# A hybrid pooling and attention layer: which scores share the PSUM banks of the row maxima

## The chip, the cores and the metric

The kernel runs on one core of one Trainium2 chip. The metric is device microseconds of one launch, taken as the median of several runs; times of one kernel agree within about 0.3%. Beside the timed runs there is one profiled execution, whose trace is read below. Times in it count from the start of its span.

## The reference, cut to what matters

One encoder layer over 1024 tokens of width 1024, in 32-bit floats. A normalised and modulated input is projected once; half of the columns go through a multi-scale mean pooling, the other half through latent attention with 8 heads, and both are joined by an output projection and added to the input. The part that the change touches is the attention of one head:

```python
def attend(qblk):
    s = jnp.einsum('bqhd,bkhd->bhqk', qblk, k, preferred_element_type=jnp.float32) * scale
    p = jax.nn.softmax(s, axis=-1)
    return jnp.einsum('bhqk,bkhd->bqhd', p.astype(v.dtype), v)
```

Queries and keys have 96 elements per head (64 without and 32 with rotary position), values 64. All 1024 positions attend to all 1024.

## The kernel before, in words

**Stages.** Until about 225 us the kernel makes the modulation, the latent projections, the pooling and the gates. From 225 to 409 us it runs the attention, in one loop over 64 jobs written out in the order in which each engine is to work (nothing is reordered by a scheduler here). From 409 us to the end it makes the rest of the output projection.

**Jobs.** A head has eight jobs, called slots here: job i belongs to head i // 8 and slot i % 8. Slots 0 to 3 (hf = 1, j = 0 to 3) each take 128 queries of the second half against all 1024 keys. Slots 4 to 7 (hf = 0, j = 0 to 3) each take 256 keys against the 512 queries of the first half, already turned round. A tile name carries the head, hf and j: `st210` is the score tile of head 2, slot 0; `st200` that of head 2, slot 4.

**One job.** Its scores are six matmuls into one PSUM tile of two banks: `scores(i, 0)` and `scores(i, 1)`, lines 800 and 804. In slots 0 to 3 DVE then takes the row maximum (lines 808 and 809). In the next turn of the loop ACT computes the exponential (line 819). For most jobs this goes to SBUF, and the PSUM tile is free when it is done. For slots 1 and 7 the exponential is written back into the PSUM tile, ACT makes its 16-bit high part (line 824) and DVE the low part (line 831), both from PSUM; only then is the tile free, about two turns after its scores. In the other slots POOL makes the low part. Six turns after the scores PE multiplies by the values (`attend`, lines 849 and 850); after slots 3 and 7 of a head ACT copies the sums out (`out_copy`, line 868) in slots 1 and 5.

**Row maxima.** Slots 4 to 7 have keys on the partitions, so their row maxima are needed ahead, for 512 queries of the next head. `prep_max` does this four times per head: two matmuls into a tile `rs` (line 730), and one DVE reduction (line 733). For heads 1, 2, 3, 5 and 7 the four stand at the ends of slots 4 to 7 of the head before; for heads 4 and 6 at the ends of slots 5, 6 and 7 of the head before and of slot 0 of the head itself. At slot 4 of heads 3, 5 and 7 an output transpose `yt` (line 887) takes the same banks first.

**PSUM.** The eight banks are shared by three pools: `stp`, two score tiles (four banks); `avp`, one tile of sums (two banks); `rsp`, one tile (two banks) for the row maxima, the transposes and, by line 793, one score tile per head. A tile that is put where another lay waits until the last reader of that one is done. `rsp` has one place, so there the tile before is always the one that is waited for. In `stp` the one of the two places that is taken is fixed when the program is built.

**Waits stand in line.** PE executes its matmuls in the order of the program. A matmul that waits for its PSUM banks holds everything behind it, other heads' sums and row maxima included.

Of the kernel before, what the change touches and what calls it, by code (L numbers as in the profile page):

```python
# [29 lines left out]
TWO_PI_PARTS = (6.28125, 0.001934051513671875, 1.255422830581665e-06, 2.430839973754928e-10)  # L30
INV_2PI = 0.15915494309189535
INP = (1, 7)
XH = 6
XS = (4, 5)
XS2 = (2, 2)
# [23 lines left out]
def body(ctx, tc, small, cond, xT, ada_sc, ada_sh, ada_gt, w_lat, w_fm, pool_w, w_uq, w_ukv, gains, pos, w_out, out):  # L59
# [148 lines left out]
    with ExitStack() as pa:  # L208
# [29 lines left out]
        for k in range(NK):  # L238
            pool, tag = (wp, "raw") if k in (0, 1, 6, 7) else (mp, wu_tags[k - 2])
# [508 lines left out]
    stp = ctx.enter_context(tc.tile_pool(name="psS", bufs=2, space=PSUM, reuse_waits="tile"))  # L748
    avp = ctx.enter_context(tc.tile_pool(name="psV", bufs=1, space=PSUM, reuse_waits="tile"))
    rsp = ctx.enter_context(tc.tile_pool(name="psR", bufs=1, space=PSUM, reuse_waits="tile"))  # L750
# [39 lines left out]
    def scores(i, n):  # L790
        h, hf, j = jobs[i]
        if n == 0:
            pool, tag = (rsp, "r") if h and hf and j == 1 else (stp, "st")
            stt[i] = pool.tile([P, 2, 512], F32, tag=tag, name=f"st{h}{hf}{j}")
        qh_, ql_ = qs[h]
        kh_, kl_ = ks[h]
        if hf == 0:
            kt = j * 2 + n
            for a, (l, r) in enumerate(((kh_, qh_), (kh_, ql_), (kl_, qh_))):
                T.matmul(stt[i][:, n], l[:HW, kt * P:(kt + 1) * P], r[:HW, 0:512], start=(a == 0), stop=(a == 2))  # L800
            return
        qt = 4 + j
        for a, (l, r) in enumerate(((qh_, kh_), (qh_, kl_), (ql_, kh_))):
            T.matmul(stt[i][:, n], l[:HW, qt * P:(qt + 1) * P], r[:HW, n * 512:(n + 1) * 512],  # L804
                     start=(a == 0), stop=(a == 2))
        if n:
            bps[i] = ep.tile([P, 1], F32, tag="bp", name=f"bp{h}{j}")
            V.tensor_reduce(bps[i], stt[i], AX.XY, ALU.max)  # L808
            V.tensor_scalar(bps[i], bps[i], nesc, 6.0 * LN2, ALU.mult, ALU.add)  # L809
# [16 lines left out]
    def in_psum(i):  # L826

        return i % 8 in INP and (i > 7 or i == 7)

# [118 lines left out]
    def at(h, step, f, *a):  # L948
        extra.setdefault((h, step), []).append((f, a))
# [3 lines left out]
    for n in range(2):  # L953
        for part in range(2):
            for d in range(2):
                at(XH + d, XS[part] + XS2[d] * n, out_split, d, (n,), (part,), G)

# [47 lines left out]
    for i in range(len(jobs) + LAG + 1):  # L1005
        live = i < len(jobs)
        h, step = i // 8, i % 8
# [14 lines left out]
        if live:  # L1022
            scores(i, 0)
# [27 lines left out]
        if live:  # L1051
            scores(i, 1)
# [141 lines left out]
```

## Time and profile before

| | |
|---|---|
| median of 3 runs | 501.46 us (501.36 to 502.86) |
| the profiled execution | 500.05 us, its span 498.3 us |
| PE, DVE, ACT, POOL busy over the span | 93%, 71%, 51%, 47% |
| first score matmul of slot 0, heads 1 to 7 | 248.92, 269.69, 290.38, 311.84, 333.03, 354.18, 374.79 us |

In a row of the timeline the first number is the start, the second how long the instruction (or a group of equal ones) is held to last, then come engine, line, operation, tiles, shape and count; in brackets how long the engine was idle before it and what ended that. `st` is a score tile, `rs` the tile of the row maxima, `p` an exponential, `ph` its parts, `av` the sums, `src` a source tile into which a row maximum is written. Matmul rows overlap: the next one may start about 0.22 us after a 512-column one whose row shows 0.38 us, so starts are compared here, and not ends of matmuls.

### The profile page before, as it was taken

Reading aid. Unit: us, or ns where it says so; the run is one execution under the profiler, and the core shown is the slowest. Engines: PE = TensorE matmul, PEld = TensorE weight load, DVE = VectorE, ACT = ScalarE, POOL = GpSimd, SP = SyncE. Lnnn points to the kernel's source line nnn. Section 1 sums busy time; section 2 is a strip of 40 time slices with the busy share of each in tenths; the row PEclk is TensorE's granted clock in tenths of the full one; section 3 lists DMA queues with packets and bytes.
Section 4 is the critical chain, followed back from the end, with each engine's and each line's share of the span. In section 5 each row is a group of like instructions: output and inputs, shape, how many; then the busy total and the mean of one; then the engine's idle time right before and its main releaser. Section 6 shows DMA issues by size and latency. Waiting matters only on the chain.

```text
span 498.3 us, 7657 instructions
## 1 busy us (share of the span) xinstructions
PE 464.9 (93%) x2956; PEld 355.0 (71%) x2956; DVE 355.9 (71%) x565; ACT 253.8 (51%) x338; POOL 234.4 (47%) x190
## 2 busy tenths in 40 slices
PE   5999998999999999999989888898898969999997
PEld 3999876898888888785555555555555658888886
DVE  4888849999999853577677887877867985913221
ACT  3756038993203030226878888888899861001000
POOL 1950040201242949448869796787869780000000
PEclk9999999999999999999999999999999999999999
DMA  8894442000102110144786779779982836753333
GB/s 300 332 307 159 171 142 65 6 1 7 47 1 91 34 58 27 57 86 95 170 148 138 162 145 176 152 151 163 224 175 63 160 113 231 276 182 129 126 128 126
DMA packets 117046, 66.33 MB, mean 133 GB/s; under 512 B 105873, under 2 KB 107793, under 8 KB 117010
## 3 DMA queue, kind: packets, MB, share of 16 engines
q1 hardware_dynamic: 117010, 65.85, 49.9%
q8 instruction: 23, 0.38, 0.3%
q14 instruction: 13, 0.11, 0.1%
HBM read 35.43 MB, written 4.19 MB: 80 GB/s over the span
## 4 chain that ended last, share of the span: by engine, by line
PE 49%; DVE 22%; ACT 10%; POOL 10%; issue 5%; DMA 3%; SPq 0%; ACTq 0%; DVEq 0%; POOLq 0%
PE ops L974 14%; PE fps L170 8%; PE st L800 4%; PE pq L548 3%; ACT ph L824 3%; PE lps L234 3%; DVE bp L808 3%; POOL fraw L152 3%; ACT p L819 3%; DMA wlr<-in_w_lat 2%; PE rs L730 2%; PE av L849 2%; PE st L804 2%; POOL s L614 2%; DVE ph L831 2%
## 5 line engine op out<-in xcount | busy, mean ns | idle before, releaser
L831 POOL TENSOR_TENSOR ph<-p,ph 128x1024 f16<-128x1024 f32 x49 | 105.9, 2168 | 13.1 <-ACT ph L824 10.2
L170 PE MATMUL fps<-xh,whi 128*128 128x512 f32 x192 | 62.0, 404 | 0.5 <-ACT whi L147 0.5
L170 PE MATMUL fps<-xh,wlo 128*128 128x512 f32 x192 | 59.3, 390 | 0.1
L170 PE MATMUL fps<-xl,whi 128*128 128x512 f32 x192 | 59.3, 390 | 0.0
L800 PE MATMUL st<-q,k 97*128 97x512 f16 x192 | 49.5, 379 | 6.7 <-ACT p L819 6.6
L804 PE MATMUL st<-k,q 97*128 97x512 f16 x192 | 48.2, 379 | 8.0 <-ACT p L819 6.4
L824 ACT ACTIVATE ph<-p 128x1024 f16<-128x1024 f32 x49 | 51.7, 1055 | 0.5
L152 POOL TENSOR_TENSOR fraw<-fraw,shift 128x1024 f32<-128x1024 f32 x7 | 22.7, 3237 | 60.8 <-DVE wlo L148 53.8
L808 DVE TENSOR_REDUCE bp<-st 128x1 f32<-128x1024 f32 x32 | 39.0, 1220 | 5.2 <-PE st L804 3.4
L170 PEld LDWEIGHTS fps<-xh,whi 128*128 128x128 f32 x192 | 35.5, 189 | 9.0 <-ACT whi L147 1.0
L170 PEld LDWEIGHTS fps<-xh,wlo 128*128 128x128 f32 x192 | 36.0, 188 | 8.1 <-DVE wlo L148 0.5
L170 PEld LDWEIGHTS fps<-xl,whi 128*128 128x128 f32 x192 | 36.1, 188 | 7.7
L935 ACT ACTIVATE owhi<-oraw 128x1024 fp32r<-128x1024 f32 (+1 forms) x10 | 8.8, 885 | 54.0 <-DMA oraw<-in_w_out 54.0
L819 ACT ACTIVATE p<-st,bp,esc 128x1024 f32<-128x1024 f32 x25 | 30.1, 1204 | 9.4 <-DVE bp L809 9.0
L804 PEld LDWEIGHTS <-q 97*128 97x128 f16 x192 | 16.6, 97 | 25.6 <-issue 10.9
L800 PEld LDWEIGHTS <-k 97*128 97x128 f16 x192 | 16.6, 97 | 21.5 <-issue 8.3
L624 ACT ACTIVATE dh<-s 128x1024 fp32r<-128x1024 f32 x4 | 4.2, 1062 | 51.9 <-DVE s L621 51.9
L819 ACT ACTIVATE p<-st,ebias,esc 128x1024 f32<-128x1024 f32 x24 | 28.9, 1203 | 2.5 <-PE st L800 1.3
L850 PE MATMUL av<-VT,ph 128*128 128x65 f16 x256 | 26.4, 193 | 2.9 <-POOL ph L831 2.9
L849 PE MATMUL av<-VT,pt 128*128 128x129 f16 x256 | 28.0, 221 | 0.8 <-DMA pt<-ph 0.8
L849 PE MATMUL av<-VT,ph 128*128 128x129 f16 x256 | 27.7, 221 | 0.2 <-DVE rb L869 0.2
L850 PEld LDWEIGHTS <-ph 128*128 128x128 f16 x256 | 22.6, 98 | 7.1 <-POOL ph L831 3.1
(297 smaller groups left out, 1142.5 us busy)
## 6 DMA issues: line engine op xcount, KB each, us to landing
fraw<-in_w_fm SPq DMA_DIRECT2D x12, 512.0 KB, 3.7
asc<-in_ada_sc SPq DMA_DIRECT2D x8, 512.0 KB, 6.0
xr<-in_xT SPq DMA_DIRECT2D x8, 512.0 KB, 5.3
ash<-in_ada_sh SPq DMA_DIRECT2D x8, 512.0 KB, 6.8
oraw<-in_w_out SPq DMA_DIRECT2D x8, 512.0 KB, 5.1
xres<-in_xT SPq DMA_DIRECT2D x8, 512.0 KB, 5.0
agt<-in_ada_gt SPq DMA_DIRECT2D x8, 512.0 KB, 5.7
out_dram<-xres SPq DMA_DIRECT2D x7, 512.0 KB, 3.0
```

Of the source, the lines that this page charges most:

```text
L152: G.tensor_tensor(pb, pb, shift.unsqueeze(2).broadcast_to([P, NK, P]), ALU.mult)
L170: T.matmul(ps[n], w[:, k, :], x_[k][:, n * 512:(n + 1) * 512], start=(k == order[0] and j == 0), stop=(k == order[-1] and j == 2))
L234: T.matmul(ps[:, :LAT], l[k][:, ts_], r[k], start=(k == 0 and i == 0), stop=(k == NK - 1 and i == 2))
L800: T.matmul(stt[i][:, n], l[:HW, kt * P:(kt + 1) * P], r[:HW, 0:512], start=(a == 0), stop=(a == 2))
L804: T.matmul(stt[i][:, n], l[:HW, qt * P:(qt + 1) * P], r[:HW, n * 512:(n + 1) * 512], start=(a == 0), stop=(a == 2))
L808: V.tensor_reduce(bps[i], stt[i], AX.XY, ALU.max)
L819: A.activation(pfs[i], st, AF.Exp, bias=bps.pop(i) if hf else ebias, scale=esc)
L824: A.activation(pas[i][:, 0], pfs[i], AF.Copy)
L831: (V if in_psum(i) else G).tensor_tensor(pas[i][:, 1], pfs[i], pas[i][:, 0], ALU.subtract)
L849: T.matmul(o_, hi, VT[:, kt, h, 0:129], start=kt == 0 and qt % 2 == 0, stop=False, skip_group_check=True)
L850: T.matmul(o_[:, 0:65], lo, VT[:, kt, h, 0:65], start=False, stop=kt == NK - 1, skip_group_check=True)
L974: T.matmul(ps[d][n], w_[:, k, :], y_[k][:, n * 512:(n + 1) * 512], start=(k == 0 and j == 0), stop=(k == NK - 1 and j == 2))
```

## The change

The table `RJ` says for each head which of slots 0 to 3 put their scores into the row maxima's banks: slots 0 and 3 in heads 1, 2, 3, 5 and 7, slot 2 alone in heads 4 and 6. Before, it was slot 1 in each of the seven. Head 0 is as it was. What `stp` holds changes by it: before, it had slots 0, 2 and 3 and the four of hf = 0, now it has slots 1 and 2 (or 0, 1 and 3) and those four.

```diff
+RJ = {1: (0, 3), 2: (0, 3), 3: (0, 3), 4: (2,), 5: (0, 3), 6: (2,), 7: (0, 3)}
...
     def scores(i, n):
         h, hf, j = jobs[i]
         if n == 0:
-            pool, tag = (rsp, "r") if h and hf and j == 1 else (stp, "st")
+            pool, tag = (rsp, "r") if h and hf and j in RJ[h] else (stp, "st")
             stt[i] = pool.tile([P, 2, 512], F32, tag=tag, name=f"st{h}{hf}{j}")
```

The number and the order of the instructions stay the same on every engine; what PE's matmuls wait for changes. (Lines after the table are two higher in the changed kernel.) Three places on PE, with the waits of each instruction; DVE, Activation (ACT) and PE name the engine waited for.

The seam between heads 1 and 2, on PE: the last row maximum for head 2 (`rs23`), sums of head 1 (`av`), and the first scores of head 2 (`st210`). Before:

```order
L730 MATMUL rs23_2565<-k2_2299,q2_2350 128x512 [waits DVE_49]
L730 LDWEIGHTS q2_2350
L730 MATMUL rs23_2565<-k2_2299,q2_2350 128x512
L849 LDWEIGHTS pt11_2431
...
L804 LDWEIGHTS q2_2350
L804 MATMUL st210_2578<-k2_2299,q2_2350 128x512 [waits Activation_49]
```

Now:

```order
L732 MATMUL rs23_2565<-k2_2299,q2_2350 128x512 [waits DVE_49]
L732 LDWEIGHTS q2_2350
L732 MATMUL rs23_2565<-k2_2299,q2_2350 128x512
L851 LDWEIGHTS pt11_2431
...
L806 LDWEIGHTS q2_2350
L806 MATMUL st210_2578<-k2_2299,q2_2350 128x512 [waits DVE_49]
```

`st210` waited for an exponential of head 1 and now waits for DVE, which reduces `rs23` in the banks that it takes over; between the two there are eight short matmuls.

Slot 4 of head 2, on PE: its scores (`st200`) and the first row maximum for head 3 (`rs30`). Before:

```order
L800 MATMUL st200_2715<-q2_2350,k2_2299 128x512 [waits Activation_49]
...
L800 LDWEIGHTS k2_2299
L800 MATMUL st200_2715<-q2_2350,k2_2299 128x512
L730 LDWEIGHTS q3_2633 [waits DMAHW0_49,DMAHW1_49]
L730 MATMUL rs30_2737<-k3_2582,q3_2633 128x512 [waits DVE_49]
```

Now:

```order
L802 MATMUL st200_2715<-q2_2350,k2_2299 128x512 [waits Activation_49]
...
L802 LDWEIGHTS k2_2299
L802 MATMUL st200_2715<-q2_2350,k2_2299 128x512
L732 LDWEIGHTS q3_2633 [waits DMAHW0_49,PE_49,DMAHW1_49]
L732 MATMUL rs30_2737<-k3_2582,q3_2633 128x512 [waits Activation_49]
```

`st200` waits for ACT in both. `rs30` waited for DVE, the last reader of slot 1, and now for ACT, the last reader of slot 3, which lies in those banks.

Head 4, on PE: the scores of slot 1 (`st411`), of slot 2 (`st412`) and of slot 4 (`st400`). Before:

```order
L804 MATMUL st411_3203<-k4_2864,q4_2915 128x512 [waits DVE_49]
...
L804 MATMUL st412_3221<-k4_2864,q4_2915 128x512 [waits Activation_49]
...
L800 LDWEIGHTS k4_2864 [waits DMAHW6_49,PE_49]
L800 MATMUL st400_3290<-q4_2915,k4_2864 128x512 [waits Activation_49]
```

Now:

```order
L806 MATMUL st411_3203<-k4_2864,q4_2915 128x512 [waits Activation_49]
...
L806 MATMUL st412_3221<-k4_2864,q4_2915 128x512 [waits DVE_49]
...
L802 LDWEIGHTS k4_2864 [waits DMAHW6_49]
L802 MATMUL st400_3290<-q4_2915,k4_2864 128x512 [waits DVE_49]
```

`st411` waited for the reduction of a row maximum and now waits for an exponential: it takes the place in `stp` in which slot 0 of the same head lies. `st412` takes the row maxima's banks. `st400` waited for the exponential of slot 2 and now waits for DVE, which reads slot 1 last.

## The prediction

> **What bounds the kernel now.** I read the page's busy shares and its chain first, then the busy times of the attention stretch, then who waits for whom on PE there, and last the timeline of one head.
>
> ```profile
> PE 464.9 (93%) x2956; PEld 355.0 (71%) x2956; DVE 355.9 (71%) x565; ACT 253.8 (51%) x338; POOL 234.4 (47%) x190
> ...
> PE 49%; DVE 22%; ACT 10%; POOL 10%; issue 5%; DMA 3%; SPq 0%; ACTq 0%; DVEq 0%; POOLq 0%
> ```
>
> PE is busiest, but the chain that ended last is only half PE. The change acts in heads 1 to 7 alone, so head 2 and the last head with the end of the attention are looked at apart (span, then busy time and count of PE, weight loads, DVE, ACT, POOL, the granted clock, the DMA share, GB/s):
>
> ```profile
> 270.00:290.40 20.40, 17.86 (x185) 10.89 (x184) 16.13 (x21) 17.38 (x19) 16.75 (x14) 1.00 0.76 151
> ...
> 374.80:409.00 34.20, 27.48 (x292) 18.99 (x289) 30.34 (x28) 29.80 (x32) 29.92 (x16) 1.00 0.46 96
> ```
>
> In a head of 20.4 us four engines work 16 to 18 us each. None fills the stretch, so the head is a ring of hand-overs, and every wait on the ring counts. PE's waits over the loop (sum, times, longest):
>
> ```profile
> PE st L800 <- ACT p L819: 6.6, 8, 1.2
> PE st L804 <- ACT p L819: 6.4, 7, 1.2
> PE st L804 <- DVE src L733: 1.6, 2, 0.9
> ```
>
> All three are waits of score matmuls for PSUM banks, the thing that the change deals out anew. The ring of head 2, by engine:
>
> ```profile
> 269.69 1.46 PE L804 MATMUL st<-k,q 97*128 97x512 f16 x6
> ...
> 275.02 1.46 PE L804 MATMUL st<-k,q 97*128 97x512 f16 x6 [1.19 <-ACT p L819]
> ...
> 280.04 0.81 PE L800 MATMUL st<-q,k 97*128 97x512 f16 x3 [0.88 <-ACT p L819]
> ...
> 289.60 0.59 PE L730 MATMUL rs<-k,q 97*128 97x512 f16 x2 [0.47 <-DVE src1h L733]
> 290.38 0.81 PE L804 MATMUL st<-k,q 97*128 97x512 f16 x3
> ```
>
> ```profile
> 272.57 0.39 ACT L868 ACTIVATE rb<-av 128x260 f32<-128x260 f32 x1 [1.04 <-PE av L850]
> 272.86 1.02 ACT L824 ACTIVATE ph<-st 128x1024 f16<-128x1024 f32 x1
> 273.76 1.21 ACT L819 ACTIVATE p<-st,bp,esc 128x1024 f32<-128x1024 f32 x1
> ...
> 276.67 1.18 ACT L819 ACTIVATE st<-st,bp,esc 128x1024 f32<-128x1024 f32 x1 [0.61 <-DVE bp L809]
> 277.87 1.02 ACT L824 ACTIVATE ph<-st 128x1024 f16<-128x1024 f32 x1
> 278.79 1.20 ACT L819 ACTIVATE p<-st,bp,esc 128x1024 f32<-128x1024 f32 x1
> ...
> 281.70 1.20 ACT L819 ACTIVATE p<-st,bp,esc 128x1024 f32<-128x1024 f32 x1 [0.62 <-DVE bp L809]
> ```
>
> ```profile
> 273.96 1.23 DVE L831 TENSOR_TENSOR ph<-st,ph 128x1024 f16<-128x1024 f32 x1 [0.47 <-ACT ph L824]
> ...
> 277.84 0.21 DVE L809 TENSOR_SCALAR bp<-bp,nesc 128x1 f32<-128x1 f32 x1
> ...
> 281.52 0.56 DVE L707 CAST src<-KT 128x768 f16<-128x768 f32 x1
> ...
> 285.09 1.23 DVE L733 TENSOR_REDUCE src1h<-rs 128x1 f16<-128x1024 f32 x1 [0.89 <-PE rs L730]
> 286.23 2.19 DVE L707 CAST src<-QT 128x768 f16<-128x768 f32 x1
> 288.33 1.21 DVE L733 TENSOR_REDUCE src1h<-rs 128x1 f16<-128x1024 f32 x1
> ```
>
> Followed round: PE does slot 0's scores (269.69) and two rounds of sums; ACT, idle for 1.04 until PE is through, copies the sums out (272.57), then makes slot 7's high part (272.86) and slot 0's exponential (273.76). DVE's low part of slot 7 (273.96) comes before the maxima of slots 1 and 2, these before the exponentials of slots 1 and 2 (276.67, 278.79); slot 4's scores stand until the latter is done (278.79 + 1.20 = 279.99; PE starts at 280.04, 0.05 later). PE goes on through two row maxima; DVE reduces the second (285.09), casts (286.23) and reduces the third (288.33 + 1.21 = 289.54); only then may the fourth be computed (289.60), and 0.78 later the next head starts (290.38). Whatever holds PE anywhere from slot 0 to slot 5 moves the rest of this ring by as much.
>
> **The change part by part.** No instruction is added, removed or moved; busy times stay. Only waits change, and a wait costs the time from when PE would have issued the matmul to when the banks come free. Where a matmul did not wait, its start in the trace is when PE was ready. A release takes 0.05 us after the reader's end, as above.
>
> Slot 0 in heads 1, 2, 3, 5, 7. It now takes the banks in which the last row maximum was just computed. First and last of the five:
>
> ```profile
> 248.77 1.23 DVE L733 TENSOR_REDUCE src1h<-rs 128x1 f16<-128x1024 f32 x1 [1.20 <-PE rs L730]
> ...
> 374.64 1.23 DVE L733 TENSOR_REDUCE src1h<-rs 128x1 f16<-128x1024 f32 x1 [1.12 <-PE rs L730]
> ```
>
> ```profile
> 248.92 1.46 PE L804 MATMUL st<-k,q 97*128 97x512 f16 x6
> ...
> 374.79 1.46 PE L804 MATMUL st<-k,q 97*128 97x512 f16 x6
> ```
>
> Free at 248.77 + 1.23 + 0.05 = 250.05, wanted at 248.92: 1.13. In head 7 375.92 against 374.79: 1.13 again. Behind the waiting matmul stand the sums for which ACT already waits, so nothing covers it: 5 x 1.13 = 5.65.
>
> Slots 1, 2 and 3 of these heads. Slot 1 takes banks long free. Slot 2 waited for slot 0's exponential (273.76 + 1.21 = 274.97); now it waits for the low part of slot 7 (273.96 + 1.23 = 275.19), 0.2 later. That is covered: its maximum is ready at 277.84 + 0.21 = 278.05, and ACT takes it at 278.79, so 0.7 is spare. Slot 3 follows slot 0's exponential, done long before. Slot 4 waits for slot 2's exponential as it did. So the wait of 1.19 is not removed, and nothing is gained: 0.
>
> The first tile after slot 3 in the row maxima's banks: `rs` at slot 4 in heads 1 and 2, the transpose `yt` in heads 3, 5, 7. Before, these banks had been left by slot 1; now by slot 3, whose exponential is the next that ACT makes after the one which releases slot 4:
>
> ```profile
> 281.69 0.59 PE L730 MATMUL rs<-k,q 97*128 97x512 f16 x2
> ...
> 302.65 1.04 PE L887 MATMUL yt<-ident,op 128*128 128x128 f32 x8
> ```
>
> ```profile
> 302.66 1.20 ACT L819 ACTIVATE p<-st,bp,esc 128x1024 f32<-128x1024 f32 x1 [0.62 <-DVE bp L809]
> ```
>
> Head 2: free at 281.70 + 1.20 + 0.05 = 282.95, wanted at 281.69: 1.26. Head 3: 303.91 against 302.65: 1.26. Both sides are moved alike by slot 0's 1.13. Slot 5, the next row maximum, DVE's cast and the fourth row maximum stand behind it: 5 x 1.26 = 6.3.
>
> Heads 4 and 6. Slot 1 no longer waits for a row maximum but for slot 0's exponential, and slot 4 for the low part of slot 1. Head 4:
>
> ```profile
> 316.00 1.46 PE L804 MATMUL st<-k,q 97*128 97x512 f16 x6 [0.87 <-DVE src L733]
> 317.61 1.46 PE L804 MATMUL st<-k,q 97*128 97x512 f16 x6 [0.16 <-ACT p L819]
> ...
> 322.64 0.81 PE L800 MATMUL st<-q,k 97*128 97x512 f16 x3 [0.87 <-ACT p L819]
> ```
>
> ```profile
> 316.35 1.21 ACT L819 ACTIVATE p<-st,bp,esc 128x1024 f32<-128x1024 f32 x1
> ```
>
> ```profile
> 317.70 1.21 DVE L808 TENSOR_REDUCE bp<-st 128x1 f32<-128x1024 f32 x1
> ...
> 321.59 1.22 DVE L831 TENSOR_TENSOR ph<-st,ph 128x1024 f16<-128x1024 f32 x1 [0.85 <-ACT ph L824]
> ```
>
> Slot 1 may start at 316.35 + 1.21 + 0.05 = 317.61 instead of 316.00: 1.61 later. Its maximum at 317.70 found DVE just free, so the chain from there to the low part (321.59 + 1.22 = 322.81) moves by 1.4 (DVE's 0.2 taken up) to 1.6, and slot 4 starts between 324.27 and 324.47 instead of 322.64: 1.6 to 1.8. I take 1.6, since DVE's last work before it is not moved. Slot 2 stands in free banks, but behind slot 1. Two heads: 3.2 (head 6 is taken as head 4).
>
> The end. POOL's last low parts decide when the output projection gets going:
>
> ```profile
> 391.47 2.41 POOL L831 TENSOR_TENSOR ph<-p,ph 128x1024 f16<-128x1024 f32 x1 [2.94 <-ACT ph L824]
> ```
>
> POOL is idle for 2.94 ahead of them, waiting for ACT, and ACT for PE: the shift goes through whole.
>
> Sum: 5.65 + 6.3 + 3.2 = 15.15 us. The profiled execution took 500.05 (span 498.3), so 515.2; the median of the runs lies 1.4 above it (501.46), so the median becomes **516.6**. The unknown is how much the other engines catch up. Lower bound: the first term is made up in the waits that follow it (510.9, rival 1); upper bound: slot 4's 1.8 in both heads and the 0.2 of slot 2 in five, 1.4 more (518.0).
>
> **The rivals.** 1. The slot 0 wait is swallowed by slot 2's wait of 1.19, which follows at once. For it: PE waits there anyway. Against: that wait ends with slot 0's exponential, behind the copy that waits for PE. It would give 516.6 - 5.65 = 510.9.
>
> 2. DVE's cast catches up. The same cast of 768 elements takes 0.56 (281.52) and 2.19 (286.23); the long one lies beside a POOL low part:
>
> ```profile
> 285.87 2.13 POOL L831 TENSOR_TENSOR ph<-p,ph 128x1024 f16<-128x1024 f32 x1
> ```
>
> Moved past it, it could be up to 1.63 shorter, and the wait before the fourth row maximum (0.47 by its row, 0.64 by starts) would vanish in heads 1 to 5: 5 x 0.64 = 3.2, 513.4. Against: POOL's part hangs on ACT and so on PE, and moves along. [...]
>
> 3. PE's clock falls. More short waits thin PE's work. By the rows above the granted clock is 1.00 in head 2 and in the last stretch, where PE is busy 27.48 of 34.20 (0.80), about as thin a load as head 2's will be (17.86 of 22.8, 0.78). At half clock seven heads would cost up to 7 x 17.86 = 125 more, some 640. [...]
>
> 4. Faster. In heads 4 and 6 slot 1 loses its wait of 0.87 and slot 2 its 0.16. Had slot 1 got the place of the earlier score tile and not slot 0's, these 1.0 per head would be won, and if the last row maxima were reduced 1.13 us sooner, slot 0 would cost nothing; then 501.5 - 2.1 = 499.4. The point from which this decides is a reduction that ends before PE reaches slot 0; it ends 1.08 after. Against it also the second term, which neither touches.
>
> 5. The change does nothing: the waits fall on tiles long free. The program's own waits (DVE at `st210`, Activation at `rs30` and `st411`) with the rows above say otherwise. 501.5.
>
> **How the numbers follow.** Forecast 0.84, rival 1 0.04, rival 2 0.04, rival 3 0.02, rival 4 0.03, rival 5 0.03. What a measurement can tell from no change is 0.3%, 1.5 us. Faster 0.03, same 0.03, slower 0.94. The range reaches down through rival 1 and up past the upper bound, with a microsecond for the runs' own spread: 510 to 519.
>
> **What would show it.** Right: slot 0's scores idle about 0.9 to 1.1 before them, ended by DVE's row maximum, in heads 1, 2, 3, 5, 7; `rs` or `yt` at slot 4 idle about 1.1, ended by ACT's exponential; slot 1 of heads 4 and 6 waiting for ACT; starts of slot 0 some 23.1 us apart from head 1 to head 3 (20.7 now); busy times as before, clock 1.00. Wrong: starts of slot 0 less than 22 us apart, which means that a wait further round the ring shrank; or slot 4's scores without a wait.

## The result and the profile after

| | before | the change |
|---|---|---|
| median | 501.36 us (500.69 to 502.86) | 517.92 us (516.43 to 519.37) |
| ratio | 1 | **1.0333**, 95% interval 1.0308 to 1.0358 |
| profiled execution, its span | 500.05, 498.3 us | 516.43, 514.6 us |

The forecast was 516.6, slower. The change run twice more, beside the experiments below, gave 516.8 (ratio 1.0322, 1.0301 to 1.0344) and 516.62 (1.0319, 1.0293 to 1.0344).

The page of the changed kernel, busy times and chain of waits:

```profile
PE 468.0 (91%) x2956; PEld 355.1 (69%) x2956; DVE 355.5 (69%) x565; ACT 253.9 (49%) x338; POOL 235.2 (46%) x190
...
PE 49%; DVE 26%; ACT 10%; POOL 9%; issue 3%; DMA 2%; SPq 0%; ACTq 0%; DVEq 0%; POOLq 0%
```

DVE, ACT and POOL work within 0.8 us as long as before. PE is busy for 3.1 us longer, half of it in head 6 (20.29 us instead of 18.70), where part of its work ran at half clock, as shown below. The rest of the 16.3 us of span is waiting, and in the chain it is DVE's share that grew, from 22 to 26%: PE now waits for DVE's reductions and low parts. The waits of PE in the attention (sum, times, longest):

```profile
PE st L806 <- DVE ph L833: 7.0, 5, 1.4
PE st L806 <- ACT p L821: 5.0, 2, 2.5
PE st L806 <- DVE src1h L735: 3.9, 4, 1.0
PE st L802 <- ACT p L821: 3.8, 6, 0.9
PE yt L889 <- ACT p L821: 3.3, 3, 1.1
PE rs L732 <- ACT p L821: 2.1, 2, 1.1
```

The first row is the old wait of slot 2, which goes by another name: low part instead of exponential. The third is slot 0's (the fifth case of it goes under `src`), the fifth and sixth are the first tile after slot 3, the second is slot 1 of heads 4 and 6. The first scores of slot 0, heads 1 to 7:

```profile
249.88 1.45 PE L806 MATMUL st<-k,q 97*128 97x512 f16 x6 [0.97 <-DVE src1h L735]
...
272.96 1.46 PE L806 MATMUL st<-k,q 97*128 97x512 f16 x6 [0.97 <-DVE src L735]
...
296.05 1.45 PE L806 MATMUL st<-k,q 97*128 97x512 f16 x6 [0.97 <-DVE src1h L735]
...
318.83 1.46 PE L806 MATMUL st<-k,q 97*128 97x512 f16 x6
...
342.81 1.46 PE L806 MATMUL st<-k,q 97*128 97x512 f16 x6 [0.97 <-DVE src1h L735]
...
365.27 1.46 PE L806 MATMUL st<-k,q 97*128 97x512 f16 x6
...
389.69 1.46 PE L806 MATMUL st<-k,q 97*128 97x512 f16 x6 [0.97 <-DVE src1h L735]
```

From start to start, with the starts before that stand ahead of the change, this gives the whole account of the span. The forecast puts each term where it falls: 1.13 at a slot 0 that waits, 1.26 at the tile after slot 3, 1.6 in heads 4 and 6.

| stretch | before | the change | longer by | forecast |
|---|---|---|---|---|
| up to slot 0 of head 1 | 248.92 | 249.88 | 0.96 | 1.13 |
| head 1 to 2 | 20.77 | 23.08 | 2.31 | 1.26 + 1.13 |
| 2 to 3 | 20.69 | 23.09 | 2.40 | 1.26 + 1.13 |
| 3 to 4 | 21.46 | 22.78 | 1.32 | 1.26 |
| 4 to 5 | 21.19 | 23.98 | 2.79 | 1.6 + 1.13 |
| 5 to 6 | 21.15 | 22.46 | 1.31 | 1.26 |
| 6 to 7 | 20.61 | 24.42 | **3.81** | 1.6 + 1.13 |
| head 7 to the end | 123.5 | 124.9 | 1.4 | 1.26 |
| sum | 498.3 | 514.6 | 16.3 | 15.15 |

Every row but one agrees within 0.2 us. (In the first row the attention itself began 0.16 earlier in this execution, at 224.96 instead of 225.12.) Head 6 is 1.1 longer than forecast. The timeline shows the ring of head 2 by engine (PE, ACT, DVE), and in the last fence PE at the waits of heads 4 and 6:

```profile
278.51 1.46 PE L806 MATMUL st<-k,q 97*128 97x512 f16 x6 [1.41 <-DVE ph L833]
...
284.31 0.81 PE L802 MATMUL st<-q,k 97*128 97x512 f16 x3
286.22 0.59 PE L732 MATMUL rs<-k,q 97*128 97x512 f16 x2 [1.10 <-ACT p L821]
```

```profile
284.97 1.21 ACT L821 ACTIVATE p<-st,bp,esc 128x1024 f32<-128x1024 f32 x1 [0.62 <-DVE bp L811]
```

```profile
271.68 1.23 DVE L735 TENSOR_REDUCE src<-rs 128x1 f16<-128x1024 f32 x1 [0.60 <-PE rs L732]
```

```profile
324.60 2.75 PE L806 MATMUL st<-k,q 97*128 97x512 f16 x12 [2.48 <-ACT p L821]
...
331.28 0.81 PE L802 MATMUL st<-q,k 97*128 97x512 f16 x3 [1.23 <-DVE ph L833]
...
371.04 4.44 PE L806 MATMUL st<-k,q 97*128 97x512 f16 x12 [2.48 <-ACT p L821]
```

Slot 0 of head 2 starts 0.05 after DVE's reduction (271.68 + 1.23 = 272.91; 272.96), the tile after slot 3 0.04 after ACT's exponential (284.97 + 1.21 = 286.18; 286.22). PE was ready for it three matmuls of 0.217 after 284.31, at 284.96: 1.26. In head 4 the 12 matmuls of slots 1 and 2 show 2.75, in head 6 4.44 for the same 12: there PE ran at half clock (granted 0.50 from 371.14 to 374.55).

### The profile page after: what moved, and what is told of

It is laid out like the page before. It is cut to its first block, busy times and chain, and to the rows that moved or that the text cites. A ratio compares the mean times of both kernels' runs of the same rounds, so it can differ in the third digit from the quotient of the medians.

```text
span 514.6 us, 7660 instructions
## 1 busy us (share of the span) xinstructions
PE 468.0 (91%) x2956; PEld 355.1 (69%) x2956; DVE 355.5 (69%) x565; ACT 253.9 (49%) x338; POOL 235.2 (46%) x190
## 4 chain that ended last, share of the span: by engine, by line
PE 49%; DVE 26%; ACT 10%; POOL 9%; issue 3%; DMA 2%; SPq 0%; ACTq 0%; DVEq 0%; POOLq 0%
PE ops L976 14%; PE fps L172 8%; PE st L806 4%; DVE bp L810 4%; PE st L802 4%; ACT ph L826 3%; PE pq L550 3%; DVE ph L833 3%; POOL fraw L154 3%; PE rs L732 3%; ACT p L821 2%; DMA wlr<-in_w_lat 2%; PE av L851 2%; PE lps L236 2%; POOL s L616 2%
## 5 line engine op out<-in xcount | busy, mean ns | idle before, releaser
L806 PE MATMUL st<-k,q 97*128 97x512 f16 x192 | 49.5, 389 | 16.8 <-DVE ph L833 7.0
L735 DVE TENSOR_REDUCE src1h<-rs 128x1 f16<-128x1024 f32 x16 | 19.6, 1225 | 11.9 <-PE rs L732 8.3
```

The lines of the kernel that those rows point to most:

```text
L735: V.tensor_reduce(s_[:, 0, qt, 0:1], ps, AX.XY, ALU.max, negate=True)
```

## The experiments

Each time stands beside runs of the kernel before on the same chip; the ratio is to those.

| kernel | median, us | ratio, 95% interval |
|---|---|---|
| heads 1, 2, 3, 5, 7 alone | 512.43 | 1.0216, 1.0195 to 1.0238 |
| heads 4 and 6 alone | 505.44 | 1.0077, 1.0058 to 1.0096 |
| slot 0 covered | 514.37 | 1.0253, 1.0224 to 1.0281 |
| tile after slot 3 covered | 511.27 | 1.0179, 1.0155 to 1.0203 |
| both covered | 509.34 | 1.0164, 1.0140 to 1.0187 |
| wait filled, operands not ready | 524.45 | 1.0472, 1.0451 to 1.0493 |
| wait filled, operands ready | 517.87 | 1.0321, 1.0295 to 1.0348 |
| before, with sums ahead | 497.33; again 497.77 | 0.9935, 0.9919 to 0.9951; 0.9943, 0.9921 to 0.9965 |
| the same, cast behind | 497.64 | 0.9938, 0.9916 to 0.9960 |

**The change in two parts.** First slots 0 and 3 in five heads, with heads 4 and 6 as before; then heads 4 and 6 alone.

```diff
-RJ = {1: (0, 3), 2: (0, 3), 3: (0, 3), 4: (2,), 5: (0, 3), 6: (2,), 7: (0, 3)}
+RJ = {1: (0, 3), 2: (0, 3), 3: (0, 3), 4: (1,), 5: (0, 3), 6: (1,), 7: (0, 3)}
```

> Heads 1, 2, 3, 5 and 7 as in the change (slots 0 and 3 in the row maxima's banks), heads 4 and 6 as before (slot 1). Ring theory (each new wait of PE is added whole to the time of its head): 5 x (1.13 + 1.26) = 11.95 us over the kernel before, 513.3 us, ratio 1.024; no wait of PE above 1.6 us in heads 1 to 6, and no half-clock stretch but the one of 3.41 us at 409 us that the kernel before has too, so a mean granted clock of 0.996 as before. Rival (the waits of heads 4 and 6 and the clock carry much of the loss): 508 us or less.

```diff
+RJ = {1: (1,), 2: (1,), 3: (1,), 4: (2,), 5: (1,), 6: (2,), 7: (1,)}
```

> Heads 4 and 6 as in the change (slot 2 in the row maxima's banks), the other five as before (slot 1). Ring theory: 2 x 1.6 = 3.2 us over the kernel before, 504.6 us, ratio 1.006. Clock theory on top (a wait of PE of 2.65 us fills most of a 3.41 us stretch, and the next 3.41 us run at half clock, as in head 6 of the changed kernel's trace): the mean granted clock falls below 0.996 in some executions, by 0.0033 for each such stretch, each costing up to 1.7 us, so 504.6 to 508 us. Rival (the clock is noise of that execution): 504.6 us and 0.996 in every execution.

The first took 512.43, its span 510.5, so 12.2 over the kernel before's (11.95 by the terms); head 2 is as long as under the whole change, 23.08. The expected ratio of 1.024 lies just above the interval. That agrees with the clock: the runs of the kernel before on that chip had a granted clock of 0.990 to 0.993, these four 0.993 to 0.996. The second took 505.44. Its head 4 is 1.66 longer than before (22.85 by starts of slot 0), as the term of 1.6 says; its head 6 is 3.2 longer. The windows of head 2 of the first and of head 6 of the second:

```profile
273.21:296.29 23.08, 18.47 (x184) 11.12 (x184) 16.43 (x20) 17.67 (x19) 17.18 (x14) 1.00 0.74 143
```

```profile
355.20:379.03 23.83, 21.34 (x190) 12.47 (x188) 15.06 (x20) 17.87 (x20) 15.39 (x12) 0.86 0.85 162
```

The second's granted clock is 0.86 over head 6, so the 1.6 above the term are again the clock. The medians' differences, 10.5 and 3.5, make 14.0 together against 16 to 16.6 for the whole; their intervals (9.8 to 11.9 and 2.9 to 4.8) just leave room for that, and the difference in clock is in it too.

**Cover for the waits.** If each wait costs its time because nothing ready stands ahead of it on PE, ready matmuls put ahead must give back just what they cover. For slot 0: the sums of that turn of the loop go ahead of its scores (for `AF0` both halves of `attend` come before `scores(i, 0)`).

```diff
-AF0 = (1, 5)
-AFL = (2, 6, 0)
+AF0 = (0, 1, 5)
+AFL = (2, 6)
```

> The changed kernel, but in slot 0 of every head the sixteen sum matmuls of that turn (0.70 us) stand ahead of slot 0's scores and not behind them, so PE works through 0.70 of the 1.13 us in which the scores wait. Ring theory: the scores still start when the row maximum is reduced, and what follows is 0.70 us shorter: 5 x 0.70 = 3.5 us under the changed kernel, 514.4 us; the wait before slot 0's scores falls to about 0.43. Rival (slot 0's wait is made up later in the head, so covering it wins nothing): 517.9 us.

For the tile after slot 3: `yt` and the row maximum of slot 4 are held back until slot 5, behind the sums of that turn.

```diff
         early(i, 0)
+        if held and step == 5:
+            h_, rh_, rsu_ = held.pop()
+            if h_ in (3, 5, 7):
+                out_tr(h_ - 2, (0, 1), rsp.tile([P, 2, 512], F32, tag="r", name=f"yt{h_}"))
+            if rsu_ is not None:
+                prep_max(rh_, rsu_)
         if live:
             scores(i, 0)
...
-        if live and step == 4 and h in (3, 5, 7):
-            out_tr(h - 2, (0, 1), rsp.tile([P, 2, 512], F32, tag="r", name=f"yt{h}"))
-        if rsu is not None:
+        if live and step == 4 and h > 0:
+            held.append((h, rh, rsu))
+        elif rsu is not None:
             prep_max(rh, rsu)
```

> The changed kernel, but the row maximum (or transpose) at the end of slot 4 of heads 1 to 7 is issued in slot 5, behind the 24 sum matmuls (1.05 us) that stood behind it. It still waits for slot 3's exponential, but 1.05 of the 1.26 us is then worked through. Ring theory: 5 x 1.0 = 5 us under the changed kernel, 512.9 us; the copy of the sums by ACT starts 1.2 to 1.7 us earlier in the head. Rival (DVE and POOL set the pace after slot 4): 517.9 us.

And both together, and beside it the change again:

> The changed kernel with both covers at once: the sums of slot 0 ahead of its scores, and the row maximum or transpose of slot 4 behind the sums of slot 5. Ring theory: the two gains add, 3.5 + 6.5 = 10 us under the changed kernel, 508 us. Rival (both covers free the same slack): 511 us, as with the second alone.

> The changed kernel once more, as the control for the three beside it on this chip: about 517.9 us and a mean granted clock between 0.983 and 0.993, as before. Both theories expect the same.

Head 2 (slot 0 to slot 0), 23.09 under the change, in the three kernels, and in the second of them the row maxima of slot 4 and slot 5:

```profile
273.39:295.78 22.39, 18.47 (x184) 11.12 (x184) 16.33 (x20) 17.66 (x19) 17.19 (x14) 1.00 0.78 148
```

```profile
272.67:294.48 21.81, 18.53 (x184) 11.18 (x184) 15.75 (x20) 17.66 (x19) 17.11 (x14) 1.00 0.77 150
```

```profile
271.81:292.94 21.13, 18.54 (x185) 11.18 (x184) 15.66 (x20) 17.67 (x19) 17.16 (x14) 1.00 0.77 155
```

```profile
285.93 0.59 PE L732 MATMUL rs<-k,q 97*128 97x512 f16 x2
286.36 1.46 PE L802 MATMUL st<-q,k 97*128 97x512 f16 x6
288.00 0.59 PE L732 MATMUL rs<-k,q 97*128 97x512 f16 x2 [0.19 <-DVE src1h L735]
```

The first cover shortens slot 0's wait from 1.13 to 0.43 and the head by 0.70. The second takes 1.03 from the wait after slot 3 (1.26 to 0.23) and 0.57 from that of the last row maximum (0.64 to 0.07), which had not been expected; since the row maximum of slot 4 now comes later, that of slot 5 waits for it, 0.34 by starts (288.00 against six matmuls of 0.217 after 286.36). 1.03 + 0.57 - 0.34 = 1.26; the head is 1.28 shorter. Both together shorten it by 1.96, where 0.70 and 1.28 make 1.98. So in this head the waits stand one after the other on one ring, and none hides in another. The medians show less: 509.34 lies 7.5 under the change's on the same chip (516.8), where the theory had 10 and its rival 6.9. The granted clock of these five executions was 0.983 to 0.986, against 0.989 to 0.990 in the change's four beside them; the profiled one had 0.985, that of the second cover alone 0.992.

**The clock: fill the long wait.** In heads 4 and 6 six matmuls that nothing uses go ahead of slot 1's scores.

```diff
+        if live and step == 1 and h in (4, 6):
+            fl = rsp.tile([P, 2, 512], F32, tag="r", name=f"fill{h}")
+            for m in range(6):
+                T.matmul(fl[:, m % 2], qs[h][0][:HW, 0:P], ks[h][0][:HW, 0:512], start=True, stop=True)
         if live:
             scores(i, 0)
```

> The changed kernel with six more matmuls of 512 columns (1.30 us) per head in heads 4 and 6, into the row maxima's banks just ahead of slot 1's scores; their results are used by nobody. They wait 1.0 us for the row maximum, work 1.30 us, and leave 0.3 us of the 2.65 us wait. Clock theory (a PE idle for most of a 3.41 us stretch gets half the clock in the next): the half-clock stretches after heads 4 and 6 are gone from the profile, the mean granted clock rises to that of a kernel without that wait (0.993 to 0.996), and the time falls by 1 to 2 us although work was added: 516 us. Rival (the clock falls for another reason, or costs nothing): 517.9 us or, with the added work, up to 520.5.

A miss. These operands are the first half of the queries, into which a transfer writes the row maxima in just that turn; the wait grew instead of being filled:

```profile
PE fill L1027 <- DMA q<-src: 6.6, 2, 3.3
```

The kernel took 524.45, at a granted clock of 0.980 to 0.990. Behind the wait of 3.29 in head 4 eleven score matmuls took 4.13, where twelve took 2.75 in head 4 of the change and 4.44, with half clock, in its head 6. The same with operands that slot 0 has read long ago:

```diff
-                T.matmul(fl[:, m % 2], qs[h][0][:HW, 0:P], ks[h][0][:HW, 0:512], start=True, stop=True)
+                T.matmul(fl[:, m % 2], qs[h][0][:HW, 512:512 + P], ks[h][0][:HW, 0:512], start=True, stop=True)
```

> The change, and in heads 4 and 6 six extra matmuls that nothing uses, ahead of slot 1's scores, with operands that have long been read by slot 0 and with a place in the row maxima's banks. They begin when the row maximum in those banks is reduced, about 0.9 us into the wait of 2.65, and take about 1.3 us, so PE is never idle for more than about 1.1 us there, and slot 1 starts when it did. Theory (the long idle waits bring the stretches at half clock): no stretch at half clock behind these two waits, mean clock 0.993 to 0.997, and 1 to 2 us less than the change on the same chip, 515 to 516. Rival (the half clock has nothing to do with these two waits): clock and time as the change's. Second rival (the matmuls put in come too late and push slot 1 back): up to 1.3 us a head more, 519.

The change beside it, on the same chip:

> The change as it is, beside the next run on one chip: 516 to 518.5 us, ratio to the kernel before 1.030 to 1.036, mean granted clock of its executions below 0.991.

On PE the fill sits in the wait of head 4, and slot 1 starts 5.77 after slot 0, as in the change (318.83 to 324.60):

```profile
320.48 1.46 PE L806 MATMUL st<-k,q 97*128 97x512 f16 x6
...
324.63 1.46 PE L1027 MATMUL fill<-k,q 97*128 97x512 f16 x6 [0.86 <-DVE src L735]
326.25 2.75 PE L806 MATMUL st<-k,q 97*128 97x512 f16 x12 [0.16 <-ACT p L821]
```

Behind it in head 4 the twelve matmuls take 2.75, as in the change, and head 6 takes 23.23 at a clock of 1.00 instead of 24.42 at 0.93. By itself that shows little: of the three profiled executions of the unfilled change one had a clock of 1.00 in head 6 too, and took 23.22 there. The median did not fall: 517.87 against 516.62. The granted clock of its six executions was 0.989 to 0.996, against 0.986 to 0.990, so it rose, but in three of them it was still 0.989. In the profiled one a stretch at half clock stood in head 5 (0.50 from 345.15 to 348.56), behind a window in which PE was busy for 1.93 of 3.42 us. So the expected gain of 1 to 2 us in the median is not shown, and why the median did not follow the clock stays open. What the traces show of the clock is in the last section.

**Sums ahead of what waits, in the kernel before.** The experiments with cover suggest the same for the waits that were there all along: the sums of slot 4's turn ahead of its scores, and in slot 7 the second half of the sums ahead of the last row maximum. `RJ` isn't in this kernel; it is the one before but for these lines.

```diff
-AF0 = (1, 5)
+AF0 = (1, 4, 5)
...
-        if rsu is not None:
+        if rsu is not None and step != 7:
             prep_max(rh, rsu)
         if av_ok and step not in AF0:
             attend(a_, 1)
             if jobs[a_][2] == 3:
                 out_copy(a_)
+        if rsu is not None and step == 7:
+            prep_max(rh, rsu)
```

> The kernel before, its banks untouched, with ready sums put ahead of two matmuls that wait: the sums of slot 4 ahead of slot 4's scores (0.70 us under a wait of 1.04), and at slot 7 the second half of its sums (0.35 us) ahead of the last row maximum (wait of 0.64). Ring theory: slot 5's scores then stand until slot 3's exponential (282.95 instead of 283.16 in head 2), 0.2 us per head from the first and 0.35 from the second in heads 1, 2 and 4; heads 3 and 5, where the transpose keeps slot 5 later, 0.66 and 0.35; heads 6 and 7 0.2 and 0.66: 4.5 us under the kernel before, 497.4 us. Rival (the head is held by the work of ACT and DVE and not by the order on PE): 501.9 us.

497.33: **faster than both kernels**, by 0.35 to 0.81% against the one before over the two intervals. Head 2 takes 20.33 instead of 20.69, its wait at slot 4 0.34 by starts instead of 1.04. Of the 4.5 us expected 3.3 came. The spans of the two profiled executions differ by 3.0, and by starts of slot 0 the missing 1.5 has two main parts. Heads 1 to 5 won 0.36 to 0.85 each, 0.7 less than expected in all. Head 6 got longer, 21.05 instead of 20.61, where 0.2 had been expected off: there sums now wait 0.50 for a transfer that turns parts of the exponential, so ACT copies the sums out 0.55 later after slot 0 (3.99 instead of 3.44), and slot 2, which waits for ACT's next exponential, starts 0.55 later too:

```profile
354.42 0.23 PE L849 MATMUL av<-VT,pt 128*128 128x129 f16 x1 [0.50 <-DMA pt<-ph]
```

For the other heads, head 2 shows it on POOL and DVE; then PE's last row maximum:

```profile
285.46 2.13 POOL L831 TENSOR_TENSOR ph<-p,ph 128x1024 f16<-128x1024 f32 x1
285.61 2.40 DVE L707 CAST src<-QT 128x768 f16<-128x768 f32 x1
...
289.19 0.59 PE L730 MATMUL rs<-k,q 97*128 97x512 f16 x2 [0.34 <-DVE src1h L733]
```

The cast came earlier beside POOL's low part and took 2.40 instead of 2.19: it ends 0.4 after that low part in both kernels (288.01 to 287.59; before, 288.42 to 288.00). The third row maximum is reduced behind it, the fourth waits for that. Hence the next: the cast behind the third row maximum.

```diff
-        if live and h + 2 < H and step > 3:
+        if live and h + 2 < H and step > 3 and step != 6:
             if step % 2 == 0:
                 conv_hi(h + 2, 3 - step // 2, V)
             conv_lo(h + 2, 3 - step // 2, G, step % 2 * 4, step % 2 * 4 + 4)
...
         if rsu is not None and step != 7:
             prep_max(rh, rsu)
+        if live and h + 2 < H and step == 6:
+            conv_hi(h + 2, 0, V)
+            conv_lo(h + 2, 0, G, 0, 4)
```

> The same with DVE's cast of slot 6, and POOL's part of it, put behind that slot's row maximum. Theory (the last row maximum waits about 0.5 us in five heads because the third is reduced behind a cast that POOL's low part beside it makes 2.2 to 2.4 us long): that wait vanishes, up to 5 x 0.5 = 2.5 us less, 495 to 496. Rival (the ring's next hand-over, ACT's copy and exponential around slot 0, takes it up, or the later cast holds up the last reduction, for which slot 1 waits): 497 to 499.

> The kernel before with slot 4's and slot 7's sums ahead of what waits, once more, beside the next run: 497 to 498 us, ratio 0.991 to 0.995.

497.64 with the cast behind and 497.77 without: no difference. PE's waits in the attention, first without and then with the cast behind:

```profile
...
PE av L849 <- DMA pt<-ph: 1.3, 2, 0.7
PE rs L730 <- DVE src L733: 1.1, 3, 0.4
PE st L804 <- DVE src L733: 0.9, 1, 0.9
PE rs L730 <- DVE src1h L733: 0.6, 2, 0.3
...
PE yt L887 <- POOL op L879: 0.2, 1, 0.2
```

```profile
...
PE av L849 <- DMA pt<-ph: 1.7, 4, 0.8
PE st L804 <- DVE src L733: 1.3, 2, 0.9
PE rs L730 <- DVE src L733: 0.9, 2, 0.4
PE yt L887 <- POOL op L879: 0.7, 1, 0.7
```

The row maxima's waits fall from 1.7 to 0.9. But the sums wait 0.4 longer for the turned low parts, the scores 0.4 longer for the last reduction, and `yt` waits 0.7 for POOL instead of 0.2: what one hand-over gives, the next takes. By starts of slot 0, heads 1 and 2 are 0.52 and 0.25 shorter and head 6 is 0.31 longer. That is the rival of this run.

## Why the prediction was right

*Slot 0, 5 x 1.13.* Right: 0.97 idle by the rows, 1.13 by starts, ended by DVE's row maximum, in heads 1, 2, 3, 5 and 7.

*First tile after slot 3, 5 x 1.26.* Right: idle for 1.10 by the row, 1.26 by starts, ended by ACT.

*Slots 1 to 3 of these heads at 0.* Right, with the turn that was worked out: slot 2 waits for the low part now, 1.57 instead of 1.35 by starts, and slot 4's wait shrinks by the same 0.2 (1.04 to 0.82).

*Heads 4 and 6, 2 x 1.6.* Right in head 4 (2.79 - 1.13 = 1.66). In head 6 the shift itself is the same: where no half clock falls in it, head 6 takes 23.22, which is 2.61 more than before, less slot 0's 1.13: 1.48. That is in the change run again, whose window of head 6 shows a clock of 1.00:

```profile
367.06:390.28 23.22, 18.60 (x190) 11.37 (x188) 16.06 (x20) 18.88 (x21) 16.50 (x12) 1.00 0.80 167
```

In the execution profiled first it took 24.42. So of the 16.3 us of span, 15.1 are the sum's, and 1.2 are the half clock in head 6. That 15.1 meets 15.15 so closely is in part luck: the rows of the table are off by -0.17 to +0.14, and these cancel.

*Every wait on the ring counts, and the end shifts whole.* Shown by the additive covers, and by the stretch from head 7 to the end, 1.4 longer for 1.26.

*Rival 1*, the wait swallowed by slot 2's: didn't happen; covering slot 0 gave 0.70 a head back, all of what it covered. *Rival 2*, the cast made shorter: in the change it took 2.19, as before, since POOL's part moved along. The tie to POOL behind it shows: in the kernel before with sums ahead the cast began 0.21 earlier beside POOL's low part and took 0.21 longer. What ties the two, no row shows. *Rivals 4 and 5*: slot 1's wait grew to 2.65, and all the waits named appeared.

*Rival 3*, the clock: this is the step that fell short. The prediction held the clock at 1.00 and argued from the mean load, 0.78 of a head. That load did not settle it. Half clock came behind single steps of 3.41 us in which PE had little to do (0.94 us of work in head 6), as the last section shows, so not seven heads at half clock came, as the rival had it, but single stretches of 3.41 us. The trace of the kernel before had one already, at 408.71 (granted 0.50); of it only the first 0.3 us lie in the last window that the prediction read, which ends at 409.00.

The runs say how much this is. In the ten runs of the change beside the experiments the mean granted clock was 0.989, in the 25 of the kernel before on the same chips 0.993, which makes about 1.2 more stretches per run (one, 3.41 us at 0.50 in 515, lowers the mean by 0.0033). Longer runs of one kernel mostly had the lower clock; a line through the times of those 25 against the clock puts a stretch at about 1.4 us (1.2 from all fifteen runs of the change). That is an estimate. By it 1.7 of the 16.2 us between the means go with the clock, and 14.5 are left, where the sum has 15.15. The same holds for the 1.4 us by which the prediction set the median above the profiled execution: it gave no reason, and in the runs of the kernel before those at a clock of 0.995 and more took 499.45 to 500.16, those at 0.990 took 502.15 to 502.81. So the times of one kernel can lie further apart than 0.3%: the first five of the change go from 516.43 (at 0.993) to 519.37 (at 0.984), which is 0.6%.

## What to carry to other kernels

Where four engines hand work round and none is full, the price of a shared buffer is the time from when the in-order engine would reach it to when its last reader is done (here 1.13 and 1.26 us); read both from the trace of before, and add the waits up if they follow one another on the ring. Work that is ready belongs ahead of an instruction that waits: it gives back what it covers (0.70 of 0.70 us in head 2), and no more than the next hand-over lets through (497.64 with the cast behind, 497.77 without). Look apart at long waits of PE, and at shorter ones close together, as they can cost clock behind them: head 6 took 1.2 us longer with half clock behind a wait of 2.65, head 5 1.6 longer with it behind a step in which PE was busy for 1.92 of 3.41 us.

## What the runs showed of the hardware

What hadn't been expected: **behind a wait of 2.65 us PE ran at half clock, in some executions and not in others**: in head 6 of the change in two of the three that were profiled. Windows of 3.41 us, first the change, then the change with the filled wait, then the kernel before (the second number is the window's length, PE's busy time comes behind it, the granted clock behind POOL's time):

```profile
367.72:371.14 3.42, 0.94 (x21) 0.84 (x18) 3.11 (x5) 2.52 (x4) 3.42 (x3) 1.00 1.10 283
371.14:374.55 3.41, 3.41 (x9) 1.21 (x8) 0.88 (x2) 0.94 (x1) 2.93 (x3) 0.50 0.56 74
```

```profile
372.45:375.86 3.41, 3.01 (x14) 1.30 (x14) 1.81 (x4) 2.87 (x3) 3.16 (x4) 1.00 1.12 159
375.86:379.28 3.42, 3.42 (x37) 2.11 (x36) 2.81 (x5) 1.88 (x2) 2.21 (x2) 1.00 0.83 189
...
341.73:345.15 3.42, 1.93 (x16) 0.95 (x15) 2.07 (x3) 3.42 (x4) 3.42 (x4) 1.00 0.71 153
345.15:348.56 3.41, 3.41 (x32) 2.59 (x31) 1.44 (x2) 0.01 (x1) 3.41 (x4) 0.50 0.71 139
```

```profile
405.30:408.71 3.41, 0.81 (x15) 0.67 (x15) 3.39 (x2) 1.72 (x2) 3.41 (x2) 1.00 0.08 11
408.71:412.12 3.41, 2.90 (x9) 2.52 (x10) 1.75 (x2) 0.00 (x0) 0.46 (x1) 0.50 0.96 352
...
251.70:255.11 3.41, 2.22 (x12) 0.89 (x10) 2.56 (x5) 3.26 (x4) 2.42 (x3) 1.00 0.85 156
255.11:258.52 3.41, 3.31 (x41) 2.24 (x40) 2.54 (x6) 2.77 (x4) 2.71 (x2) 1.00 0.82 154
```

Behind windows with 0.94, 1.93 and 0.81 us of work on PE comes one at half clock, behind those with 3.01 and 2.22 none. The 1.93 lies at the seam of heads 4 and 5, where no wait of 2.65 is; in the same place the trace of the change has two shorter waits close together, of 0.53 and 0.97 us (before the rows at 340.90 and 342.81). In the traces of the two kernels the stretches at half clock start on one grid each: in the change at 371.14, 425.75 and 514.50, which is 16 and 26 steps of 3.413 us apart, in the kernel before at 408.71 and 497.46, 26 such steps apart. So these two traces were cut along their grids, and PE's busy share worked out for each step from 10 us on that was at full clock itself. After all five steps with PE busy for less than 0.5 of the step (0.06 to 0.35) came a step at half clock, after none of the 281 above (0.52 and more). Two of the five stand just before the end of an execution. In windows of other runs half clock came after shares of 0.42 (1.44 us, heads 4 and 6 alone) and 0.44 (1.49 us, the change run a third time), and after 0.56 twice (1.92 us in that run, 1.93 with the filled wait), though in the two traces above it came after neither 0.52 (at 81.00 in the change) nor 0.56 (1.91 us, at 81.03 in the kernel before).

Where the grid lies differs from execution to execution: 345.15 with the filled wait is 7.6 steps from 371.14 in the change. In the change the wait of head 6 falls into one step, the one with 0.94 us of work, and half clock comes behind it; the wait of head 4, as long, lies across two, with 2.18 and 2.17 us of work (319.94 to 323.35 to 326.77), and none comes. Where one stretch at half clock fell into a head, it took 1.2 and 1.6 us longer: head 6 24.42 with it and 23.22 without, head 5 24.09 with it and 22.47 without. With heads 4 and 6 alone the half clock lasted for two steps (0.50 from 360.46 to 367.29), though PE's rows fill 2.90 of the first; these rows don't say why.
